# Neighbourhood-attention and Fourier encoder layer: first token tiles gated from Y in place, prompt weight remainders on VectorE, three small reorderings

## The chip, the core and the metric

The kernel runs on one core of one Trainium2 chip. The time is device microseconds for one execution. Before the change the median of 3 runs is 946.03 us (943.36 to 946.63).

The core's engines work side by side, each on its own queue of instructions in order: TensorE (in the profile PE for the matmuls, PEld for the loading of weights), VectorE (DVE), ScalarE (ACT), GpSimd (POOL), and SyncE (SP), which here does nothing but issue DMAs.

## The reference

One encoder layer is applied to a prompt of 256 tokens and a sample of 2048 tokens, each of width 1024, with the same weights. All arrays are float32.

```python
def rms_norm(x, g):
    inv = lax.rsqrt(jnp.mean(x * x, axis=-1, keepdims=True) + RMS_EPS)
    return x * inv * g

def fourier_mix(u, w_f, b_f):
    ug = u.reshape(b, s, F_GROUPS, F_GROUP_DIM)            # 8 groups of 64
    spec = jnp.fft.fft2(ug, axes=(1, 3), norm='ortho')
    return spec.real.reshape(b, s, F_WIDTH) @ w_f + b_f    # width 512

def encoder_layer(x, w_in, rpb, w_fourier, b_fourier, g_pre, g_na, g_f, w_out, g_post):
    h = rms_norm(x, g_pre)
    q, k, v, z_a, u_f, z_f = split(h @ w_in)               # six parts of width 512
    y_a = neighbourhood_attention(q, k, v, rpb)            # 8 heads of 64, windows of 8 x 16 on a grid 64 wide
    y_f = fourier_mix(u_f, w_fourier, b_fourier)
    mixed = jnp.concatenate([rms_norm(y_a, g_na) * jax.nn.silu(z_a),
                             rms_norm(y_f, g_f) * jax.nn.silu(z_f)], axis=-1)
    return x + rms_norm(mixed @ w_out, g_post)
```

## The kernel before

**Products.** Every operand of a large product is kept as a high part (a copy in the type fp32r, mostly made by ScalarE) and a remainder (operand minus high part, mostly made by VectorE). A product is then three matmuls: high by high, high by remainder, remainder by high (`mm3`, L171 to L174). Results come into one of eight PSUM banks, which are dealt out by tag: three banks "a", two "b", one "c", two "t".

**Stages.** Prompt and sample are one row of 2304 tokens (`T`), the prompt first (`TP` = 256).

1. *Prompt stage, to about 125 us.* The projections v and u of the prompt and of two blocks of the sample are made by steps `c` (loop at L706). `x_split(c)` splits a token tile; `diag` and `diag_group` write the tokens' norm factors on diagonals (ScalarE, L327), which PE transposes into rows (`spread`, L321) for the scaling of later tiles. `r_sum` (L467) makes sums of weights on VectorE. Then 16 steps `b` make the other projections of the prompt, one weight block of 128 x 1024 each. `b_raw` (L575) splits the block two steps ahead: copy on ScalarE (L578), remainder (L579) on VectorE or, for the four steps of `WP`, on GpSimd. Beside that VectorE scales token tiles (`n_scale`, L417), adds them (`n_sum`, L440) and splits them (`n_first`, L446), and at the end splits the first weights of the next stage (`op_split`, L495).
2. *Sample projections, to about 555 us.* Seven products of half blocks stand for eight, for each of 16 weight pairs.
3. *Fourier mix, to about 610 us.* After the transform along tokens, `y_mm(e, ti)` (L1248) makes one of four channel blocks `e` and one of three column blocks `ti`, taken in the order 2, 0, 1, in two banks. `y_out` (L1262) copies the first bank with the bias by ScalarE (L1264), and VectorE puts sums and differences with the second bank in place in Y (L1272), a tile of 128 channels x 2304 tokens. The prompt's 256 tokens come out of `ti` = 2 (L1296 and L1297). Y goes to DRAM (`yD`), its squares are added up for the norm (ScalarE and GpSimd, L1332 to L1340). In the last block, `e` = 3, the scores of the first two attention groups, `G[0]` and `G[1]`, lie between the products.
4. *Attention and the Fourier half of the output, to about 847 us.* 36 groups (4 head pairs x 9) run in a pipeline of steps `k`: `transp` (L1479) transposes a group's weights by PE into the banks `ptb` and copies them to SBUF, `scores` (L1162) makes the next group's logits, `bias_max` and `exps` the softmax, `pv` the product with v, `run_squares` the squares for the norm. In every second step `f_mm` (L1442) multiplies a tile of 128 tokens of gated Y by the lower half of `w_out`, in two halves of 512 columns (12 matmuls each), and `f_evac` (L1453) scales them by the norm's factor, which `f_norm` (L1465) has summed by PE.
5. *Attention half and residual, to the end.* 18 tiles: `a_mm`, `evac` (L1678), the last norm and `residual` (L1707); the last tile is written out in `last_tile` (L1719).

**The first token tiles.** Tile 0 (tokens 0 to 127) is not loaded like the others. The prompt part of each Y goes to `yD` (L1298). In block `e` = 2 the first three blocks of tile 0 are loaded back into `y0` (L1317) with the gate Z (L1318), and GpSimd multiplies them (L1320); the fourth block is multiplied by VectorE straight from Y (L1349). ScalarE copies the high part (L1351), VectorE makes the remainder (L1353), together `y0h`. Then `y0` is loaded again for tile 1 (L1357 and L1358), which GpSimd gates later (L1409). `f_mm` of tile 0 uses `ptb[0]` for its first half and the bank "c" for its second.

**What sets the order.** PE's order is that of the program text everywhere. On ScalarE, VectorE, GpSimd and SyncE it is that of the text in the stages 1 and 2 (L602 to L961) and from the last Y block on (L1342); in between a planner orders them by its own costs and priorities. A tile of a pool waits for a free slot: Y has three slots, the squares of L1339 two.

## Time and profile before

| | |
|---|---|
| median of 3 runs | 946.03 us (943.36 to 946.63) |
| the profiled execution | 947.1 us, of which its span from first to last instruction is 945.3 us |
| mean granted TensorE clock | 0.995 of full speed |
| VectorE, ScalarE, GpSimd busy | 670.4, 470.3, 343.7 us |
| DMA | 265.02 MB, mean 280 GB/s |

A row of a timeline holds: start in us, length in us, engine, line of the program, operation, the tile written <- the tiles read (buffer numbers left out), partitions x elements and type, the count if rows are merged, and in brackets the engine's idle time just before, with what ended it. A length is that of one instruction from its start to its end; the next of the same engine often starts a little earlier, since instructions overlap by about 0.1 us. For merged rows the length runs over all of them. Matmuls overlap more: 128x512 ones start about 0.23 us apart and are 0.39 us long at full clock. "issue" is a wait for nothing that the profile shows. The chain of waits is followed back from the last instruction, at each step to what released it.

### The profile page before, as it was taken

How to read it: one execution, taken by the hardware profiler on the slowest of the kernel's cores; microseconds unless marked ns; L12 is line 12 of the kernel's file. 1: busy time of each engine (PE TensorE's matmuls, PEld its weight loads, DVE VectorE, ACT ScalarE, POOL GpSimd, SP SyncE). 2: the span in 40 equal slices, each digit the busy share in tenths (PEclk: the TensorE clock that was granted, in tenths of full speed). 3: DMA queues.
4: the chain of work that ended last, by engine and by line, in shares of the span. 5: the costliest groups of instructions: out<-in, count | busy, mean ns of one | idle time of the engine just before them, and what ended most of it. 6: DMA issues, size and time to landing. Idle time of an engine off the chain costs nothing.

```text
span 945.3 us, 18908 instructions
## 1 busy us (share of the span) xinstructions
PE 929.2 (98%) x6790; PEld 777.4 (82%) x6790; DVE 670.4 (71%) x1304; ACT 470.3 (50%) x1038; POOL 343.7 (36%) x340
## 2 busy tenths in 40 slices
PE   9999999999999999999999999899999999999996
PEld 7879988888888888888888898778787887888885
DVE  5468998687864977597666545568666665659997
ACT  5747577633232643233344326457556666654443
POOL 2201302436650300363343100445456565424444
PEclk9999999999999999999999999999999999999999
DMA  8899767468573999759979788779788899869993
GB/s 307 324 354 386 242 230 299 154 247 312 205 288 151 357 396 354 275 188 324 326 275 312 256 312 280 284 232 274 243 243 271 267 288 284 268 228 373 339 344 125
DMA packets 146861, 265.02 MB, mean 280 GB/s; under 512 B 21896, under 2 KB 86664, under 8 KB 144016
## 3 DMA queue, kind: packets, MB, share of 16 engines
q1 hardware_dynamic: 146608, 263.79, 80.5%
q8 instruction: 54, 0.88, 0.4%
q14 instruction: 39, 0.32, 0.1%
q10 hardware_dynamic: 160, 0.02, 0.0%
HBM read 175.21 MB, written 95.88 MB: 287 GB/s over the span
## 4 chain that ended last, share of the span: by engine, by line
PE 83%; DMA 3%; DVE 1%; issue 1%; ACT 0%; POOL 0%; DVEq 0%; SPq 0%; ACTq 0%
PE mm L173 15%; PE mm L174 15%; PE mm L172 15%; PE ptb L1432 11%; PE po L1432 10%; PE pv L1511 5%; PE ptb L1489 3%; PE s L1181 2%; PE pab L1007 2%; PE ptb L1181 2%; DMA yD<-Y 1%; DMA wo<-woD 1%; DMA vr<-wv 0%; DMA y<-yD 0%; PE pz L174 0%
## 5 line engine op out<-in xcount | busy, mean ns | idle before, releaser
L172 PE MATMUL mm<-xh,wa 128*128 128x512 f32 x448 | 174.4, 389 | 0.0
L174 PE MATMUL mm<-xh,wa 128*128 128x512 f32 x448 | 174.3, 389 | 0.0
L173 PE MATMUL mm<-xl,wa 128*128 128x512 f32 x448 | 174.3, 389 | 0.0
L172 PEld LDWEIGHTS mm<-xh,wa 128*128 128x128 f32 x448 | 84.1, 188 | 17.5
L174 PEld LDWEIGHTS mm<-xh,wa 128*128 128x128 f32 x448 | 84.1, 188 | 17.4
L173 PEld LDWEIGHTS mm<-xl,wa 128*128 128x128 f32 x448 | 84.1, 188 | 17.4
L1432 PE MATMUL ptb<-wo,yh 128*128 128x512 f32 x272 | 86.8, 400 | 0.0
L1432 PE MATMUL po<-w,yh 128*128 128x512 f32 x280 | 86.8, 391 | 0.0
L1215 POOL TENSOR_SCALAR w<-w,m 128x352 f32<-128x352 f32 (+4 forms) x136 | 75.3, 573 | 30.7 <-PE s L1181 14.2
L549 POOL TENSOR_TENSOR ws<-wr 128x512 f32<-128x512 f32 x16 | 21.4, 1338 | 176.8 <-DMA wr<-wz 160.1
L564 DVE TENSOR_TENSOR wa<-wr,wa 128x512 fp32r<-128x512 f32 x60 | 59.9, 1005 | 31.2 <-ACT wa L563 31.2
L1208 ACT ACTIVATE w<-w,m 128x352 f32<-128x352 f32 (+4 forms) x136 | 69.9, 521 | 13.2 <-DVE m L1203 12.9
L863 DVE TENSOR_TENSOR f<-u,mm 128x512 f32<-128x512 f32 x64 | 43.6, 681 | 35.1 <-PE mm L174 30.4
L173 PE MATMUL mm<-vl,xh 128*128 128x512 f32 x168 | 65.6, 390 | 0.2 <-DVE vl L495 0.2
L174 PE MATMUL mm<-vh,xl 128*128 128x512 f32 x168 | 65.4, 389 | 0.0
L172 PE MATMUL mm<-vh,xh 128*128 128x512 f32 x168 | 65.4, 389 | 0.0
L1432 PEld LDWEIGHTS ptb<-wo,yh 128*128 128x128 f32 x272 | 49.3, 188 | 14.8 <-ACT sqa L1539 3.1
L1432 PEld LDWEIGHTS po<-w,yh 128*128 128x128 f32 x280 | 52.3, 188 | 11.0
L563 ACT CAST wa<-wr 128x512 fp32r<-128x512 f32 x60 | 36.6, 617 | 45.5 <-PE mm L174 22.1
L1511 PEld LDWEIGHTS pv<-pt,v 96*64 96x64 f32 (+2 forms) x1280 | 45.2, 137 | 11.6 <-issue 6.6
L1432 PE MATMUL po<-w,yl 128*128 128x512 f32 x140 | 54.5, 389 | 0.0
L1432 PE MATMUL ptb<-wo,yl 128*128 128x512 f32 x136 | 53.1, 390 | 0.0
(252 smaller groups left out, 2208.1 us busy)
## 6 DMA issues: line engine op xcount, KB each, us to landing
wr<-wz SPq DMA_DIRECT2D x48, 512.0 KB
vl<-sD SPq DMA_DIRECT2D x20, 512.0 KB
xm<-xm SPq DMA_DIRECT2D x9, 1024.0 KB
oD<-ofs SPq DMA_DIRECT2D x18, 512.0 KB
of<-oD SPq DMA_DIRECT2D x18, 512.0 KB
yr<-yD SPq DMA_DIRECT2D x34, 256.0 KB
zD<-f SPq DMA_DIRECT2D x16, 512.0 KB
woD<-wo SPq DMA_DIRECT2D x16, 512.0 KB
```

What stands on the lines that cost most here:

```text
L172: nc.tensor.matmul(out, lh, rh, start=first, stop=False)
L173: nc.tensor.matmul(out, lh, rl, start=False, stop=False)
L174: nc.tensor.matmul(out, ll, rh, start=False, stop=last)
L563: nc.scalar.copy(o[:, 0], src)
L564: nc.vector.tensor_tensor(out=o[:, 1], in0=src, in1=o[:, 0].bitcast(F32), op=ALU.subtract)
L863: nc.vector.tensor_tensor(out=dst(f, b), in0=src(uu[u]), in1=src(p), op=op)
L1181: nc.tensor.matmul(sp[2 * b + h][64 * y:64 * y + 64, j * w:(j + n) * w], g["q"][hs, 128 * b + 64 * y:128 * b + 64 * y + 64], kk[hs, k:k + ...
L1208: nc.scalar.activation(w, w, AF.Exp, bias=m[:, h:h + 1], scale=-1.0, accum_out=m[:, 2 + h:3 + h])
L1215: nc.gpsimd.tensor_scalar(w, w, m[:, 4 + h:5 + h], 1.0, ALU.mult, ALU.mult)
L1432: nc.tensor.matmul(p, (d["l"] if x == 2 else d["h"])[:, c], w(n, int(x == 1), c), start=j == 0, stop=j == 11)
L1489: nc.tensor.transpose(ptb[2 * b + y][:nk, x:x + 64], g["w"][b][ys, h, c0:c0 + nk], ident[ys, ys])
L1511: nc.tensor.matmul(p[hs, b, o], v[:nk, b, x, hs], g["pt"][b][:nk, h, j * 128 + o.start:j * 128 + o.stop], start=first, stop=last)
```

## The change

The change has five parts.

- The tile `y0` holds both prompt tiles (256 tokens) and stays in SBUF. Z for both is loaded once, before the first Y block; GpSimd multiplies each of the blocks 0 to 2 from Y as soon as the block's `ti` = 2 is out, VectorE the fourth. The stores of Y's prompt part, the loads of it, and the second load of Z are gone; tile 1 is gated with tile 0.
- `WP` is gone: the remainders of the steps 7, 9, 11 and 13 of the prompt are made on VectorE.
- In step `c` = 3 `x_split` of the next tile stands ahead of the diagonals.
- The first half of tile 0 in `f_mm` uses a bank "a", from which scores take theirs, in place of `ptb[0]`. In three steps of the pipeline (`k` = 9, 19, 27), where `run_squares` stands ahead of `transp`, the two copies of `transp` change engines.
- In `last_tile` the second residual of the tile before stands between the two last evacuations, and not behind both.

```diff
--- before.py
+++ after.py
@@ -26,7 +26,6 @@
 NG = 13
 NK = 16
 BP = (3, 5)
-WP = (7, 9, 11, 13)
 
 HALF = ((0, 28), (4, 8), (12, 16), (20, 24))
 KW = (24, 32, 32, 24)
@@ -576,7 +575,7 @@
         wh, wl = [gt(BS, F32R, "w" + x) for x in "hl"]
         src = wp_[b]
         nc.scalar.copy(wh, src)
-        (nc.gpsimd if b in WP else nc.vector).tensor_tensor(out=wl, in0=src, in1=wh.bitcast(F32), op=ALU.subtract)
+        nc.vector.tensor_tensor(out=wl, in0=src, in1=wh.bitcast(F32), op=ALU.subtract)
         wb[b] = wh, wl
 
 
@@ -707,12 +706,11 @@
     for c in range(3, 6):
         if c < 5:
             wz_load(3)
+        if c < 5:
+            x_split(c + 1)
         if c == 3:
             diag(0, 2)
             diag_group(0)
-        if c < 5:
-            x_split(c + 1)
-        if c == 3:
             for q in range(8):
                 r_sum(q)
         if c == 4:
@@ -1236,7 +1234,8 @@
     pg = ExitStack()
     sm = pg.enter_context(tc.tile_pool(name="smY", bufs=2))
     sqy = pq_.enter_context(tc.tile_pool(name="sqy", bufs=1, side="right"))
-    y0 = sqy.tile([128, 2, 4, 128], F32, name="y0")
+    y0 = sqy.tile([128, 2, 4, TP], F32, name="y0")
+    nc.sync.dma_start(y0[:, 1], zD[0, :, :TP].rearrange("(c p) t -> p c t", p=128))
     for t, (g, x) in enumerate(zip(G, (0, 512))):
         g["w"] = []
         for w in g["kw"]:
@@ -1295,7 +1294,6 @@
             comb(Y[:, TP + 1024:TP + 1025], slice(256, 257), ALU.subtract)
             comb(Y[:, 0:129], slice(257, 386), ALU.subtract)
             comb(Y[:, 255:128:-1], slice(258, 385), ALU.add)
-            nc.sync.dma_start(yD[1, e, :, :TP], Y[:, :TP])
 
     def first_soft(g, f=None):
         if f:
@@ -1313,11 +1311,8 @@
         if e < 3:
             for ti in (2, 0, 1):
                 y_out(e, ti, *y_mm(e, ti))
-                if e == 2 and ti == 2:
-                    nc.sync.dma_start(y0[:, 0, :3], yD[1, :3, :, :128].rearrange("c p t -> p c t"))
-                    nc.sync.dma_start(y0[:, 1], zD[0, :, :128].rearrange("(c p) t -> p c t", p=128))
-                if e == 2 and ti == 0:
-                    nc.gpsimd.tensor_tensor(out=y0[:, 0, :3], in0=y0[:, 0, :3], in1=y0[:, 1, :3], op=ALU.mult)
+                if ti == 2:
+                    nc.gpsimd.tensor_tensor(out=y0[:, 0, e], in0=Y[:, :TP], in1=y0[:, 1, e], op=ALU.mult)
             nc.sync.dma_start(yD[1, e, :, TP:], Y[:, TP:])
             if e == 0:
                 load_wo1(1)
@@ -1346,16 +1341,14 @@
         py = y_mm(e, 0)
         y0h = gt([128, 2, 4, 128], F32R, "y0h")
         y0h = [y0h[:, 0], y0h[:, 1]]
-        nc.vector.tensor_tensor(out=y0[:, 0, 3], in0=Y[:, :128], in1=y0[:, 1, 3], op=ALU.mult)
+        nc.vector.tensor_tensor(out=y0[:, 0, 3], in0=Y[:, :TP], in1=y0[:, 1, 3], op=ALU.mult)
         sq = sm.tile([128, SQ], F32, tag="sqf", name="sqf", bufs=2)
-        y_out(e, 0, *py, lambda: (nc.scalar.copy(y0h[0], y0[:, 0]),
+        y_out(e, 0, *py, lambda: (nc.scalar.copy(y0h[0], y0[:, 0, :, :128]),
                                   nc.scalar.activation(sq[:, :TP], Y[:, :TP], AF.Square)))
-        nc.vector.tensor_tensor(out=y0h[1], in0=y0[:, 0], in1=y0h[0].bitcast(F32), op=ALU.subtract)
+        nc.vector.tensor_tensor(out=y0h[1], in0=y0[:, 0, :, :128], in1=y0h[0].bitcast(F32), op=ALU.subtract)
         soft(G[0], 0)
         soft(G[0], 1)
 
-        nc.sync.dma_start(y0[:, 0], yD[1, :, :, 128:256].rearrange("c p t -> p c t"))
-        nc.sync.dma_start(y0[:, 1], zD[0, :, 128:256].rearrange("(c p) t -> p c t", p=128))
         scores(G[1])
         py = y_mm(e, 1)
         first_soft(G[1])
@@ -1440,8 +1433,11 @@
         nc.sync.dma_start(d["xt"], A["xn"][d["t"] * 128:d["t"] * 128 + 128, :])
 
     def f_mm(d, n):
-        p = d["p", n] = ptb[n if d is ftiles[0] else 2 + n] if n == 0 or d is not ftiles[0] else \
-            ps.tile([128, 512], F32, tag="c", name="pf", bufs=1)
+        if d is ftiles[0]:
+            p = ps.tile([128, 512], F32, tag="ac"[n], name="pf", bufs=3 - 2 * n)
+        else:
+            p = ptb[2 + n]
+        d["p", n] = p
         out_mm(d, n, range(12), p, lambda n, x, c: wo1[n][c][:, x])
 
     def a_mm(d, n):
@@ -1476,7 +1472,7 @@
         n = len(ds)
         rsq_ops(inva[:, ds[0]["i"]:ds[0]["i"] + n], p[:, :n], n, 1.0 / 512)
 
-    def transp(g):
+    def transp(g, swap=False):
         g["pt"] = []
         for b, ch in enumerate(g["ch"]):
             m = len(ch)
@@ -1488,7 +1484,8 @@
                         ys, x = slice(64 * y, 64 * y + 64), 64 * (h * m + j)
                         nc.tensor.transpose(ptb[2 * b + y][:nk, x:x + 64], g["w"][b][ys, h, c0:c0 + nk], ident[ys, ys])
             ov = o.rearrange("p h (j y x) -> p y h j x", y=2, x=64)
-            for y, copy in ((0, nc.scalar.copy), (1, V.tensor_copy)):
+            for y in range(2):
+                copy = V.tensor_copy if swap != (y > 0) else nc.scalar.copy
                 copy(ov[:z, y, :, :m], ptb[2 * b + y][:z, :128 * m].rearrange("p (h j x) -> p h j x", h=2, x=64))
             g["pt"].append(o)
 
@@ -1556,12 +1553,11 @@
            6: [(Y2, 1664, 2304), (Y, 1110, 1708)], 8: [(Y, 1708, 2304)]}
     ftiles[0]["h"], ftiles[0]["l"] = y0h
     y_parts(ftiles[1])
-    ftiles[1]["raw"], ftiles[1]["z"] = y0[:, 0], y0[:, 1]
+    ftiles[1]["raw"] = y0[:, 0, :, 128:]
     for x in (slice(TP, TP + 512), slice(TP + 512, T)):
         nc.sync.dma_start(yD[1, 3, :, x], Y[:, x])
     f_mm(ftiles[0], 0)
     f_norm(range(2))
-    ys_mul(ftiles[1])
     ptb += [ps.tile([128, 512], F32, tag="b", name="ptb", bufs=2) for x in range(2)]
     for x in range(2, 4):
         V.memset(ptb[x], 0.0)
@@ -1593,9 +1589,10 @@
             y = k - 24
             nc.sync.dma_start(WO[y % 2][:, y // 2].bitcast(F32), woD[0, y % 2, y // 2])
         x = k // 2
-        if k % 2 and g and i < 2:
+        first = bool(k % 2 and g and i < 2)
+        if first:
             run_squares()
-        transp(f)
+        transp(f, first)
         run_squares()
         if k % 2:
             if g:
@@ -1729,7 +1726,8 @@
                 factor(b)
                 residual(b, 0)
             evac(d, p, ns, 1 + 2 * q)
-        residual(b, 1)
+            if q == 0:
+                residual(b, 1)
         sa = d["sa"]
         V.tensor_scalar(sa[:, 0:1], sa[:, 0:1], sa[:, 1:2], None, ALU.add)
         part_sum(sa)
```

## The prediction

> **What bounds the kernel now.** I read the page's first part, then the windows, the chain of waits, and the timelines of single engines where the chain leaves TensorE (PE). The page says that PE is the bound: 16.1 of 945.3 us are without a matmul, so a change can win only in those pauses, or where PE runs slower than it could.
>
> ```profile
> PE 929.2 (98%) x6790; PEld 777.4 (82%) x6790; DVE 670.4 (71%) x1304; ACT 470.3 (50%) x1038; POOL 343.7 (36%) x340
> ```
>
> The windows show where the largest pause is (columns: stretch, its length, then busy time and count of PE, PEld, DVE, ACT, POOL, then the granted clock, DMA share, GB/s):
>
> ```profile
> 608.00:610.00 2.00, 0.39 (x3) 0.06 (x1) 0.00 (x0) 0.00 (x0) 0.61 (x1) 1.00 0.24 77
> 610.00:612.00 2.00, 0.00 (x0) 0.00 (x0) 0.94 (x4) 0.94 (x2) 0.38 (x1) 0.72 0.00 0
> 614.00:616.00 2.00, 2.00 (x6) 1.60 (x5) 1.28 (x6) 0.62 (x3) 0.83 (x3) 0.50 0.47 137
> 616.00:618.00 2.00, 2.00 (x8) 1.55 (x7) 0.00 (x0) 0.00 (x0) 0.94 (x1) 0.57 0.70 272
> ```
>
> PE stands still, the clock falls to 0.50, and work that comes afterwards runs at half rate. PE's own timeline says what that work is:
>
> ```profile
> 608.05 0.34 PE L174 MATMUL py<-abh,pql 128*128 128x384 f32 x1
> 612.53 5.40 PE L1432 MATMUL ptb<-wo,y0h 128*128 128x512 f32 x12 [4.14 <-issue]
> 617.77 0.50 PE L1468 MATMUL pfn<-ones,sqs 128*128 128x1 f32 x4
> 618.13 3.01 PE L1432 MATMUL pf<-wo,y0h 128*128 128x512 f32 x12
> 621.32 0.47 PE L1489 MATMUL ptb<-ident,sc 64*128 64x64 f32 x8 [0.18 <-DVE ofs L1463]
> ```
>
> The first token tile's first twelve matmuls start 4.14 us after the last y matmul and take 5.40 us; the same twelve for the other half, at full clock, take 3.01. The chain of waits (start, us, what) names the cause, a round trip of Y through DRAM:
>
> ```profile
> 596.65 8.90 DMA yD<-Y
> 605.63 3.69 DMA y<-yD
> ```
>
> **The changes, part by part.** *The first tile from Y.* Removed: four stores of Y's prompt part, its two loads, the gating at L1320 and L1409. Added: GpSimd gates each of the first three Y tiles where it stands (L1336's 128x256 operation, 0.73 us, is the same shape), and one load of both prompt tiles of Z ahead of them. When are the split halves of tile 0 (y0h) ready then? These rows hold the chain:
>
> ```profile
> 603.28 1.33 DVE L1272 TENSOR_TENSOR Y<-t,py 128x252 f32<-128x252 f32 x7
> 606.60 1.08 DVE L1272 TENSOR_TENSOR Y<-t,py 128x384 f32<-128x384 f32 x3
> 604.33 0.56 ACT L1264 ACTIVATE t<-py,bfs 128x384 f32<-128x384 f32 x1
> 606.38 0.29 DVE L1349 TENSOR_TENSOR y<-Y,y 128x128 f32<-128x128 f32 x1 [1.77 <-DMA y<-zD]
> 610.41 0.62 ACT L1351 CAST y0h<-y 128x512 fp32r<-128x512 f32 x1 [5.52 <-POOL y L1320]
> 611.06 0.69 DVE L1353 TENSOR_TENSOR y0h<-y,y0h 128x512 fp32r<-128x512 f32 x1 [3.39 <-ACT y0h L1351]
> 600.42 0.73 POOL L1336 TENSOR_TENSOR sqs<-sqs,sqf 128x256 f32<-128x256 f32 x1
> ```
>
> GpSimd's last operation ends at 601.15 and would end 0.73 later, 601.9, with the third gate behind it. The fourth gate, on VectorE, starts when the Y sums end (604.6), not at 606.38, since Z is there long before. It is twice as wide: at most twice 0.29, so done by 605.2. The copy on ScalarE takes 0.62 (605.8); beside it VectorE makes the next block's Y sums, 1.08 (606.3), and then the remainder, 0.69: y0h is complete at about 607.0. PE needs it at 608.05 plus 0.2, the spacing of these matmuls, so 608.25. The wait is gone with 1.2 us to spare. The bank must be free too: the change gives the first half a bank of the score pool, whose last user is evacuated by ScalarE (L1264) by 604.9.
>
> Without a pause there is no fall of the clock, so the first twelve take what the second twelve do. From start to start: idle 612.53 - 608.25 = 4.28; first half 617.77 - 612.53 = 5.24 against about 2.75 (3.01 less the tail of the last matmul), 2.49; and the transposes, which waited at 621.32 for the evacuation of a bank that they share no more, come about 0.3 earlier, at 614.2. Together **7.1 us**. What is late next is that same evacuation:
>
> ```profile
> 620.42 0.76 DVE ofs L1463
> ```
>
> It started 2.65 after the norm matmuls of 617.77. These move to 611.0, so it ends near 614.4. The scores behind the transposes take three banks of the pool in which it now lies, and start at about 614.65: 0.2 us to spare, hidden but barely; if it slips by x, I lose x - 0.2. I take the full 7.1; the ends are 5 (a 2 us wait left) and 7.4.
>
> *How the clock is counted.* In the windows the half rate lasts to about 617.6, 5 us after the matmuls resume. [...]
>
> *The prompt remainders.* Four splits of a 128x1024 weight go from GpSimd to VectorE, which in this stage has hardly a gap:
>
> ```profile
> 103.23 3.27 POOL L579 TENSOR_TENSOR wl<-wr,wh 128x1024 fp32r<-128x1024 f32 x1 [2.71 <-ACT wh L578]
> 108.99 3.07 POOL L579 TENSOR_TENSOR wl<-wr,wh 128x1024 fp32r<-128x1024 f32 x1 [2.49 <-ACT wh L578]
> 104.27 4.38 DVE L440 TENSOR_TENSOR nx<-nx 128x2048 f32<-128x2048 f32 x1
> 109.71 4.50 DVE L440 TENSOR_TENSOR nx<-nt,nx 128x2048 f32<-128x2048 f32 x1
> 114.25 2.29 DVE L440 TENSOR_TENSOR nx<-nx 128x2048 f32<-128x2048 f32 x1
> 116.45 1.22 DVE L579 TENSOR_TENSOR wl<-wr,wh 128x1024 fp32r<-128x1024 f32 x1
> 117.73 0.39 PE L174 MATMUL mm<-ph,wl 128*128 128x256 f32 x1 [1.34 <-DVE wl L579]
> 124.40 0.50 PE L173 MATMUL mm<-vl,xh 128*128 128x512 f32 x1 [0.22 <-DVE vl L495]
> ```
>
> Added: four times 1.14 (1.22 less the overlap with the next), 4.56 us on VectorE, with PE waiting behind it twice. Given back: the two sums of 4.38 and 4.50 are the same shape as the one of 2.29, and each ends just 2.15 after a GpSimd split ends (103.23 + 3.27 = 106.50, and 108.65; 108.99 + 3.07 = 112.06, and 114.21). I read this as VectorE standing still while GpSimd works. Without these splits both return to 2.29: 4.30 us. Net, VectorE is 0.26 later.
>
> [...]
>
> *x_split ahead of the diagonals.* Here PE waits for a remainder that is queued behind ten diagonals on ScalarE:
>
> ```profile
> 48.95 3.02 ACT L327 ACTIVATE dg<-onesq,invt 128x128 f32<-128x128 f32 x10
> 52.95 1.23 DVE L296 TENSOR_TENSOR xl<-xr,xh 128x1024 fp32r<-128x1024 f32 x1 [10.36 <-ACT xh L293]
> 54.23 0.50 PE L174 MATMUL mm<-wc,xl 128*128 128x512 f32 x1 [0.53 <-DVE xl L296]
> ```
>
> The remainder comes some 3 us earlier, the diagonals 1 us later, near 53.0. PE transposes them ahead of the product that waited, so it waits for the last of them instead: of 0.7 us lost I count 0.2 won. VectorE's eight sums start 3 us earlier too, but the remainder at 78.9 waits for ScalarE and a store, so between 0 and 1.1 us of that lead lives. Both parts together, PE at 124.4: from 0.5 late (the 0.26, and short waits at single weights) to 0.9 early; I take **0.1 won**.
>
> *Copies exchanged.* In three steps ScalarE squares the previous group before it copies the bank that the next scores need; one of them:
>
> ```profile
> 730.63 1.02 DVE L1492 COPY pt<-ptb 128x384 f32<-128x384 f32 x2
> 730.90 0.84 ACT L1492 COPY pt<-ptb 128x384 f32<-128x384 f32 x2
> 731.43 0.43 PE L1181 MATMUL ptb<-kk,q 64*64 64x256 f32 x1
> ```
>
> ScalarE's first copy ends at 731.32. VectorE's would end at 731.14: 0.2 earlier, and both engines are still done before the products that read all four copies. Three steps, **0.6 us**, ends 0 and 0.7.
>
> *Last residuals.* The earlier tile's second half moves ahead of the last small evacuation. VectorE's row at the end (the 128-wide evacuation is the one before):
>
> ```profile
> 938.32 0.74 DVE L1714 SCALAR_TENSOR_TENSOR of<-ptb,sr,of 128x512 f32<-128x512 f32 x1
> 938.71 0.19 ACT L1683 ACTIVATION_READ_ACCUMULATOR jk<-of 128x1 f32 x1
> 938.98 0.20 DVE L1734 TENSOR_SCALAR sa<-sa 128x1 f32<-128x1 f32 x1
> ```
>
> The final sum at 938.98 waited for ScalarE (938.90) as much as for the residual. The moved residual fits into the half microsecond that VectorE waited for PE and pushes the evacuation back by less than 0.1. I take 0, ends 0.1 lost and 0.2 won.
>
> **Sum.** 7.1 + 0.1 + 0.6 + 0 = 7.8 us. The profiled execution took 947.1 (span 945.3 and 1.8 around it), so 939.3; the median of the three runs, 946.03, lies 1.07 below it. On that median: 946.03 - 7.8 = **938.2 us**.
>
> **Rivals.** *VectorE becomes the bound of the prompt stage.* If the two long sums have another cause than GpSimd, nothing returns, and the 4.56 stand in a chain that ends at PE's wait of 124.40. For it: VectorE has no gap there. Against it: the two ends at the same distance. Time: 938.2 + 4.5 = 942.7.
>
> *A shorter wait takes the old one's place.* The third gate is behind GpSimd's adds, the copies are behind ScalarE's squares, and the evacuation has only 0.2 us. Say 2 us of waiting in all: 940.2. The clock would not fall, since here it fell only about 2.5 us into the pause (0.72 on average over 610 to 612).
>
> *Slower: the first gate waits for Z.* The planner lays out GpSimd's queue here. The first gate stands ahead of the eight adds of squares, ScalarE's squares wait for these adds, and the copy that frees PE's banks is queued behind them.
>
> ```profile
> 595.06 5.39 POOL L1340 TENSOR_TENSOR sqs<-sqs,sqf 128x288 f32<-128x288 f32 x7 [2.52 <-ACT sqf L1339]
> 581.83 1.42 SPq L1159 DMA_DIRECT2D za<-zD  x2
> 597.95 0.37 SPq L1318 DMA_DIRECT2D y<-zD  x1
> ```
>
> If Z came as late as it does now (606.3, when L1349 starts), the adds would follow two gates later, at 607.8 in place of 595.06, 12.7 us late. PE has little work in hand without free banks, some 0.7 us by my estimate: 12 us idle, and 2.5 for the clock, so 938.2 + 14.5 = 952.7. It decides at about 593.6, two gates before the seven adds. Against it: in the text of this stage the load follows the za loads, which SyncE has issued by 583.3, and the 8.4 us that it takes now (597.95 to 606.3) would end at 591.7.
>
> *The change doesn't do what it says:* something else holds the first tile as long as the load did, its weights or its bank. Nothing in the trace is that late; both are there by 605.
>
> **Chances.** Forecast 0.80; VectorE bound 0.08; a shorter wait 0.08; slower 0.03; no effect 0.01. A measurement here can tell about 0.5% from no change, 4.7 us: faster is under 941.3, slower over 950.8. The forecast's own ends, (5 or 7.4) with the small terms' ends, and 1 us for the medians (the three runs span 3.3), give 936 to 941. The range reaches up to VectorE as the bound: 936.0 to 942.8. Faster: 0.80 and most of the shorter wait, 0.86; same: 0.10; slower: 0.04.
>
> **What would show it.** Right: the windows near 608 to 614 show PE full and the clock at 1.00; the first tile's first twelve take about 3 us; no load of y from yD in the chain; L440's sums all take 2.3; the scores in the three steps start about 0.2 after their predecessors' end. Wrong: a pause of PE of over 1 us after the y matmuls, sums of L440 that still take over 4, PE's wait near 117 to 124 grown by microseconds, or GpSimd's adds starting after 595.

## The result, and the profile after

The kernel after takes 939.0 us (median of 4 runs, 937.48 to 939.44) against 946.33 (943.36 to 946.97): ratio 0.9926, interval 0.9902 to 0.995. That is 7.3 us less; forecast were 7.8 and 938.2. The profiled execution of after took 937.48 us, with a span of 935.7.

The page's first part, the row that answers to the first one of before. TensorE (PE) has 10.4 us without a matmul instead of 16.1:

```profile
PE 925.3 (99%) x6790; PEld 774.5 (83%) x6790; DVE 669.9 (72%) x1308; ACT 469.8 (50%) x1038; POOL 332.0 (35%) x337
```

The windows of after where PE stood still before (columns as in the prediction: PE, PEld, DVE, ACT, POOL, clock, DMA share, GB/s):

```profile
606.00:608.00 2.00, 2.00 (x11) 1.69 (x10) 0.87 (x5) 1.63 (x7) 1.50 (x4) 1.00 0.04 8
608.00:610.00 2.00, 2.00 (x12) 1.70 (x12) 1.00 (x7) 0.32 (x2) 0.00 (x0) 1.00 0.14 53
```

PE is full and the clock stays at 1.00; DMA is at 0.04 and 0.14: little is moved. The timeline of after over that stretch:

```profile
602.73 0.43 DVE L1344 TENSOR_TENSOR y<-Y,y 128x256 f32<-128x256 f32 x1
...
603.19 0.62 ACT L1346 CAST y0h<-y 128x512 fp32r<-128x512 f32 x1 [0.23 <-DVE y L1344]
...
604.07 0.68 DVE L1348 TENSOR_TENSOR y0h<-y,y0h 128x512 fp32r<-128x512 f32 x1
...
606.21 2.92 PE L1425 MATMUL pf<-wo,y0h 128*128 128x512 f32 x12
608.97 0.50 PE L1464 MATMUL pfn<-ones,sqs 128*128 128x1 f32 x4
609.33 3.03 PE L1425 MATMUL pf<-wo,y0h 128*128 128x512 f32 x12
...
611.72 0.75 DVE L1459 TENSOR_SCALAR ofs<-pf,invf 128x512 f32<-128x512 f32 x1
612.29 0.46 PE L1485 MATMUL ptb<-ident,sc 64*128 64x64 f32 x8
```

The last gate, the copy and the remainder are done at 604.75, 1.5 us before PE comes to the tile. The first half's twelve matmuls take 2.92, the second half's 3.03: no half rate. The evacuation ends at 612.47 and the scores behind the transposes start at 612.68: 0.21 to spare, where 0.2 was forecast.

Where the time went, by the starts of the same matmuls in the two profiled executions:

| stretch (times of the kernel before) | before | after | difference |
|---|---|---|---|
| start to the first product at full clock (9.99) | 9.99 | 8.42 | -1.57 |
| from there to the product with the prompt's last late remainder, for which PE waits on VectorE (117.73) | 107.74 | 107.01 | -0.73 |
| to the last y product (608.05) | 490.32 | 490.60 | +0.28 |
| to the first matmul of the first tile (612.53) | 4.48 | 0.18 | -4.30 |
| to the norm matmuls (617.77) | 5.23 | 2.76 | -2.47 |
| to the transposes (621.32) | 3.55 | 3.32 | -0.23 |
| to 661.7 | 40.38 | 40.56 | +0.18 |
| to 874.2 (holds the three exchanged steps) | 212.47 | 212.14 | -0.33 |
| to the last matmul (937.74) | 63.57 | 63.58 | +0.01 |
| to the end of the span | 7.56 | 7.13 | -0.43 |

The first row is the same code in both. The second needs other runs to be read: the experiments below hold the same code several times.

### The profile page after: what moved, and what is told of

It reads as the page before. It is cut to its first block, busy times and chain, and to the rows that moved or that the text cites. A ratio compares the mean times of both kernels' runs of the same rounds, so it can differ in the third digit from the quotient of the medians.

```text
span 935.7 us, 18895 instructions
## 1 busy us (share of the span) xinstructions
PE 925.3 (99%) x6790; PEld 774.5 (83%) x6790; DVE 669.9 (72%) x1308; ACT 469.8 (50%) x1038; POOL 332.0 (35%) x337
## 4 chain that ended last, share of the span: by engine, by line
PE 94%; DMA 3%; DVE 2%; issue 1%; ACT 0%; DVEq 0%; SPq 0%
PE mm L172 18%; PE mm L173 18%; PE mm L171 17%; PE ptb L1425 10%; PE po L1425 10%; PE pv L1508 5%; PE ptb L1485 3%; PE s L1179 3%; PE pab L1005 2%; PE ptb L1179 2%; DMA woD<-wo 1%; PE py L171 1%; PE py L173 1%; PE py L172 1%; PE pf L1425 1%
## 5 line engine op out<-in xcount | busy, mean ns | idle before, releaser
L563 DVE TENSOR_TENSOR wa<-wr,wa 128x512 fp32r<-128x512 f32 x60 | 57.7, 969 | 30.6 <-ACT wa L562 30.3
```

The lines of the kernel that those rows point to most:

```text
L563: nc.vector.tensor_tensor(out=o[:, 1], in0=src, in1=o[:, 0].bitcast(F32), op=ALU.subtract)
```

## The experiments

My theory: all of the gain that a median shows is the first tile's, by the wait, the half clock behind it and the shared bank; of the small parts only the exchanged copies and the moved residual win anything. Rivals: the first-tile gain was made elsewhere; the prompt stage won by the change; the bank, not Y, held the tile.

**The first tile alone.** The kernel after with the other parts undone.

```diff
+WP = (7, 9, 11, 13)
...
-        nc.vector.tensor_tensor(out=wl, in0=src, in1=wh.bitcast(F32), op=ALU.subtract)
+        (nc.gpsimd if b in WP else nc.vector).tensor_tensor(out=wl, in0=src, in1=wh.bitcast(F32), op=ALU.subtract)
...
-        transp(f, first)
+        transp(f)
...
-            if q == 0:
-                residual(b, 1)
+        residual(b, 1)
```

> The kernel after the change with every part undone but the first token tiles from Y (with the new bank). My theory: the main pause of TensorE and its half clock are this part alone, so the transposes of the first group start 7.0 us earlier than in the kernel before, counted from the last y product, and the prompt stage, the steps of the exchanged copies and the tail stand as before; 7.0 us less than before in all. Rival, that part of the gain at the transposes was made elsewhere (engines that run earlier since the prompt stage): under 6.5 here.

Measured: 939.0 us (938.55 to 940.06) against 946.07, ratio 0.9933 (0.9918 to 0.9948): as much as all parts together. From the last y product to the transposes 6.26 us, to the hundredth what after takes. The forecast's main part is this part's own. The prompt stage, with the old code, also took 107.13 instead of the 107.74 of the profile of before, so most of the 0.73 in the table above is scatter between executions.

**All other parts.** The kernel before with the prompt remainders on VectorE, the split ahead of the diagonals, the exchanged copies and the moved residual.

> The kernel before with all other parts: prompt remainders on VectorE, the split ahead of the diagonals, exchanged copies, moved residual. My theory: 0.4 to 0.8 won in the prompt stage, 0.6 in the three steps, 0.5 in the tail, so 1.5 to 1.9 less than before (counted in the trace from the first full-rate matmul on), and the pause of about 4.1 us and the half clock at the first token tile stay. By my prediction's terms it would be 0.7. Rival, that the moved residual wins nothing and the tail's 0.45 is scatter between runs: the time from the last matmul's start to the end of the span stays as before.

Measured: 945.56 us (942.71 to 946.91), ratio 0.9994 (0.9983 to 1.0005): the size is inside what can be told from no change. The trace tells the parts apart. Tail: 6.97, so 0.59 less than before; the three steps' stretch: 212.03, 0.44 less. The prompt stage took 108.31, longer than with the old code: I had expected 0.4 to 0.8 won there, and that is wrong. The pause stayed, but it cost less than in the profile of before; PE's rows:

```profile
613.62 4.52 PE L1430 MATMUL ptb<-wo,y0h 128*128 128x512 f32 x12 [4.12 <-issue]
617.98 0.50 PE L1466 MATMUL pfn<-ones,sqs 128*128 128x1 f32 x4
```

The pause is as long as before (4.12 and 4.14), but the twelve matmuls take 4.52 instead of 5.40. The clock is the reason; it is taken up below.

**The bank alone.** The kernel before, with the first half in a bank of the scores.

```diff
-        p = d["p", n] = ptb[n if d is ftiles[0] else 2 + n] if n == 0 or d is not ftiles[0] else \
-            ps.tile([128, 512], F32, tag="c", name="pf", bufs=1)
+        if d is ftiles[0]:
+            p = ps.tile([128, 512], F32, tag="ac"[n], name="pf", bufs=3 - 2 * n)
+        else:
+            p = ptb[2 + n]
+        d["p", n] = p
```

> The kernel before with the new bank alone for the first half of the first token tile. In the kernel before, that half's bank is read by the softmax's maximum until 612.42, and its first matmul starts at 612.53. My theory: the operands are there at 611.75 (end of VectorE's remainder), so the first matmul starts 0.5 to 0.8 earlier, and the transposes, which shared the bank, lose their wait of 0.18: 0.5 to 1.0 won. Rival, that the first half waited for its operands alone, as I put it in the prediction: 0.2 to 0.3 won, all at the transposes.

Measured: 944.92 us (943.25 to 947.8), ratio 0.9991 (0.9978 to 1.0003). Its timeline:

```profile
608.85 0.62 ACT L1351 CAST y0h<-y 128x512 fp32r<-128x512 f32 x1 [5.47 <-POOL y L1320]
609.50 0.69 DVE L1353 TENSOR_TENSOR y0h<-y,y0h 128x512 fp32r<-128x512 f32 x1 [3.37 <-ACT y0h L1351]
...
609.52 4.57 PE L1432 MATMUL pf<-wo,y0h 128*128 128x512 f32 x12 [2.64 <-ACT y0h L1351]
```

The first half starts as soon as ScalarE's copy is done, and VectorE's remainder comes in time behind it. In the kernel before the copy was done at 611.03 and PE started at 612.53, just behind the end of this row of VectorE (612.42; in the run "The clock by itself" below the wait's own row names the maxima, `DVE m L1203`):

```profile
612.07 0.35 DVE L1203 CUSTOM_DVE_ANT_1 sc<-ptb,tb 128x192 f32<-128x192 f32 x1
```

So 1.5 us of the pause of 4.14 was the old bank, which the softmax's maxima still read, queued on VectorE behind the tile's remainder. From the last y product to the transposes it is 10.69 against 13.26: 1.50 of that is the bank, 0.83 a shorter half rate (taken up below), 0.25 the transposes' wait. I had expected 0.5 to 0.8 here; the mechanism is right and larger, and the rival, that the tile waited for its operands alone, falls. It is what my prediction had taken for granted.

**After with the old bank.**

```diff
-            p = ps.tile([128, 512], F32, tag="ac"[n], name="pf", bufs=3 - 2 * n)
+            p = ps.tile([128, 512], F32, tag="c", name="pf", bufs=1) if n else ptb[0]
```

> The kernel after with the first token tile's first half back in its old bank. In the kernel before with the new bank alone, the first half started 1.5 us earlier against its operands than with the old one, whose last reader is the softmax's maximum. My theory: with Y gated in place the operands are so early that this reader has ended (605.76 in the kernel after) before TensorE comes to the tile (606.21), so the start stays; the transposes, which share the old bank, wait for its evacuation (612.47) and start 0.2 to 0.4 later: 0.2 to 0.4 slower than after. Rival, that the bank is a part of the 7 us by itself: the first half starts over 1 us later than after.

Measured: 938.04 us (937.77 to 939.07), ratio 0.9924 (0.9907 to 0.9941). The two rows of its timeline that matter:

```profile
611.79 0.75 DVE L1459 TENSOR_SCALAR ofs<-ptb,invf 128x512 f32<-128x512 f32 x1
...
612.69 0.46 PE L1485 MATMUL ptb<-ident,sc 64*128 64x64 f32 x8 [0.26 <-DVE ofs L1459]
```

The first half starts 0.18 behind the last y product, as in after: no wait for the bank. The transposes wait 0.26 for the evacuation and come 0.32 later than in after, and 0.12 of that is made good at the next scores. A bank that was worth 1.5 us while Y came late is worth 0.2 once Y is early: the two gains overlap, and neither can be read off by undoing one part alone.

**The clock by itself.** The kernel before with matmuls in the pause whose result is not used.

```diff
+    wm = ps.tile([128, 512], F32, tag="a", name="wm", bufs=3)
+    for x in range(17):
+        nc.tensor.matmul(wm, wo1[0][0][:, 0, :128], wo1[0][1][:, 0], start=True, stop=True)
```

> The kernel before with 17 matmuls of 128x512 added between the last y product and the first token tile, whose result nobody uses (some 3.9 us at 0.23 each): TensorE is busy through the pause, but the first token tile still comes when Y comes back from DRAM. My theory: the clock stays at 1.00, the first twelve matmuls of the tile take 2.7 to 3.0 instead of 5.4, and the kernel is 2.0 to 2.5 us faster than before although it does more. Rival A, that the first twelve are slow for another cause (their operands or weights come late one by one): they still take over 5 us and the time stays as before. Rival B, that only part of the half rate is the pause's doing: 1 to 1.5.

PE's timeline in that run:

```profile
606.90 4.05 PE L1560 MATMUL wm<-wo,wo 128*128 128x512 f32 x17
611.28 2.97 PE L1432 MATMUL ptb<-wo,y0h 128*128 128x512 f32 x12 [0.32 <-DVE m L1203]
...
696.61 0.69 PE L1181 MATMUL s<-kk,q 64*64 64x256 f32 x1 [2.46 <-issue]
```

The tile comes as late as before (4.55 behind the last y product), and its first twelve matmuls take 2.97 instead of 5.40. Start to start that is 5.23 to 2.81: 2.42 won by nothing but a busy PE. Rivals A and B fall. The whole kernel did not show it: 945.38 us (943.95 to 949.46), ratio 1.0 (0.9987 to 1.0013). The last row shows where the profiled execution lost it again: 85 us later PE stands still for 2.46 us with nothing visible to wait for, and the granted clock falls again (0.50 from 696.3 to 703.2); the stretch from 661.7 to 874.2 takes 218.33 there against 212.47. That execution, with 949.46 us, is the slowest of the ten, and what the others lost is not seen. Why PE stands still is open (see the next run).

**Bank and busy pause together.** The same with the new bank and 11 such matmuls.

> The kernel before with the new bank for the first half and 11 matmuls of 128x512 (2.5 us) ahead of it whose result nobody uses. With the new bank alone TensorE still stood still for 2.64 us and the first twelve matmuls took 4.4 at half clock; with 17 such matmuls and the old bank they took 2.8. My theory: bank (1.5) and clock (1.6) add up, what stays is the wait for Y's way through DRAM alone (2.6 to 2.9), so from the last y product to the transposes 9.0 to 9.2 instead of 13.3 in the kernel before and 6.3 in the kernel after; about 3.5 to 4 faster than before. Rival, that the clock falls even in a row of such matmuls or that the bank's gain was scatter: over 10.5 to the transposes.

From the last y product to the transposes 9.53 us (expected 9.0 to 9.2; before 13.26, after 6.26), so bank and clock add up to 3.7, and 3.3 is left for Y's way through DRAM. The median is 945.02 us (942.61 to 950.33), ratio 0.9993 (0.9979 to 1.0007): again less than the trace promised. The profile shows 0.64 lost at the next scores and 1.19 near 694, at nearly the same matmul as in the run before, again under "issue". The kernels before and after show no stall there (PE busy 10.00 of 10.00 us from 690 to 700). The cause was not shown.

**Remainders on GpSimd, beside other work.** After with the steps 7 and 9 on GpSimd again.

```diff
+WP = (7, 9)
...
-        nc.vector.tensor_tensor(out=wl, in0=src, in1=wh.bitcast(F32), op=ALU.subtract)
+        (nc.gpsimd if b in WP else nc.vector).tensor_tensor(out=wl, in0=src, in1=wh.bitcast(F32), op=ALU.subtract)
```

> The kernel after with the prompt remainders of the steps 7 and 9 on GpSimd again; they run beside VectorE's scaling of token tiles and splits, the two of steps 11 and 13 beside the sums stay on VectorE. My theory, that GpSimd and VectorE block each other in operations with two operands in SBUF: all sums take 2.3; two splits of 1.14 less on VectorE, some of it given back where a split on GpSimd meets one on VectorE; TensorE's waits between 97 and 125 us, 1.0 in all, shrink to 0.3 to 0.8, and the product of v at the stage's end comes that much earlier. Rival, that any work of GpSimd there costs VectorE as much as it takes over: the stage ends as in the kernel after.

**The same with the steps 11 and 13** (`WP = (11, 13)`).

> The kernel after with the prompt remainders of the steps 11 and 13 on GpSimd again, those beside VectorE's sums. My theory: two of the sums take 4.4 and 4.5 again, VectorE has 4.3 more for the sums and 2.3 less for the splits, and the product of v at the stage's end comes up to 2 us later than in the kernel after. Rival, that the long sums have another cause: all sums 2.3 and the stage ends 0.3 to 1 earlier, like the run with steps 7 and 9.

With 7 and 9: 936.28 us (934.8 to 938.02), ratio 0.9902 (0.9883 to 0.9922). Its timeline, one of the two steps:

```profile
95.62 1.22 DVE L579 TENSOR_TENSOR wl<-wr,wh 128x1024 fp32r<-128x1024 f32 x1
96.06 3.05 POOL L579 TENSOR_TENSOR wl<-wr,wh 128x1024 fp32r<-128x1024 f32 x1 [2.90 <-ACT wh L578]
96.76 2.72 DVE L417 SCALAR_TENSOR_TENSOR nx<-nx,gpre,iv 128x512 f32<-128x512 f32 x4
```

GpSimd's split runs beside VectorE's scaling, whose second operand `iv` is in PSUM, and the four take 2.72 in all, 0.68 each, against 1.40 for two with no split beside them (86.13): VectorE is not held up. All sums take 2.3 (the view of groups: `L440` 2288, 2287 and 2285 ns), and PE has no wait between 90 and 140 us. The expectation was too small: counted from the last u product's evacuation, the product of v comes 2.27 earlier than in after (44.90 against 47.17), not 0.3 to 0.8.

With 11 and 13: 941.64 us (939.94 to 942.52), ratio 0.9956 (0.994 to 0.9973). Its timeline:

```profile
100.55 1.23 DVE L579 TENSOR_TENSOR wl<-wr,wh 128x1024 fp32r<-128x1024 f32 x1
101.31 4.92 POOL L579 TENSOR_TENSOR wl<-wr,wh 128x1024 fp32r<-128x1024 f32 x1 [73.27 <-ACT wh L578]
101.69 2.29 DVE L440 TENSOR_TENSOR nt<-nx 128x2048 f32<-128x2048 f32 x1
...
104.01 4.36 DVE L440 TENSOR_TENSOR nx<-nx 128x2048 f32<-128x2048 f32 x1
...
107.39 3.22 POOL L579 TENSOR_TENSOR wl<-wr,wh 128x1024 fp32r<-128x1024 f32 x1 [1.17 <-ACT wh L578]
108.30 3.40 DVE L579 TENSOR_TENSOR wl<-wr,wh 128x1024 fp32r<-128x1024 f32 x1
...
111.75 0.58 PE L174 MATMUL mm<-ph,wl 128*128 128x256 f32 x1 [2.33 <-DVE wl L579]
```

Read it as turns. GpSimd's split, begun at 101.31, meets VectorE's remainder, which runs until 101.78; VectorE's sum, begun at 101.69, still goes ahead of it, to 103.98, and the split ends only at 106.23. VectorE's next sum, begun at 104.01, ends 2.14 later, at 108.37. GpSimd's second split ends at 110.61, 2.24 behind that, and VectorE's remainder, 1.22 by itself, takes 3.40 and ends 1.09 behind it. PE waits 2.33 for that. In these rows one of the two stands still until the other is through, and not always the one that began second. GpSimd stands still in the other runs too: each of the twelve splits in the rows of before, of the first tile alone and of the two runs here ends 2.24 to 2.29 behind the end of a VectorE operation with both operands in SBUF (99.11 and 96.84 in the run with the steps 7 and 9). I read that as its own length, an estimate from these ends; the rest of the 2.90 to 4.92 recorded is then waiting.

The rival (long sums of another cause) falls, and my 2 us were too small: the product of v comes 2.94 later than in after (50.11 from the last u product's evacuation, against 47.17). Measured from the same evacuation to PE's last late remainder, the stage takes 44.35 against 40.48 in after and 39.02 with the steps 7 and 9. Not all of that is VectorE's: behind the pause of 2.33 PE's first matmul is recorded with 0.58, the same shape behind the pause of 1.34 in the kernel before (117.73) with 0.39. How much of the lateness is PE's was not shown.

**An earlier lead for VectorE.** After with the split of the third weight block ahead of ScalarE's evacuation of the last u product.

```diff
         p_mm("u", c, range(4))
+        if c == 5:
+            b_raw(2)
...
-        if b < 14:
+        if 0 < b < 14:
             b_raw(b + 2)
```

> The kernel after with the split of the prompt's third weight block (copy on ScalarE, remainder on VectorE) ahead of ScalarE's evacuation of the last u product, which is TensorE's to end: in the kernel after VectorE stands still for 5.85 us behind that, and the lead of the moved token split, 2 us there, is lost. My theory: VectorE's remainder starts some 5 us earlier (near 71 instead of 76.6), keeps a lead up to 110, and TensorE's four waits of 0.2 and what waits at 115 to 122 go: the product of v 0.8 to 1.1 earlier, and the kernel 0.8 to 1.1 faster than after. Rival, that loads of weights hold VectorE next: the lead is gone by 100 and the time is that of after.

First two timelines of the kernel after, VectorE and ScalarE, which show where the lead of the moved token split ends:

```profile
74.95 0.69 ACT L350 ACTIVATE uo<-mm,invt 128x512 f32<-128x512 f32 x1 [5.16 <-DMA vN<-vo]
75.53 1.04 ACT L577 CAST wh<-wr 128x1024 fp32r<-128x1024 f32 x1
...
76.60 1.23 DVE L578 TENSOR_TENSOR wl<-wr,wh 128x1024 fp32r<-128x1024 f32 x1 [5.85 <-ACT wh L577]
```

ScalarE is free for `uo` some 2 us earlier than with the old order and waits there. My expectation called that a wait for PE; the row names the store of `vo`, and the row is right: PE ended the u product at 73.7, 1.2 us earlier. `uo` goes into the slot of the `vo` one step before, whose store was issued at 66.77 and let go 8.2 us later; with the old order (the run of the first tile alone) it was issued at 68.75 and let go 6.3 us later, at 75.09. The lead is lost in a store that takes longer by as much. The DMA engines are full there in both runs (share 0.98 to 1.07 from 62 to 76 us in after, 1.00 and 0.98 from 60 to 70 and to 80 with the old order). `uo` starts 66.3 to 68.0 us after PE's first product at full clock in eight runs with the new order, 66.3 to 67.2 in five with the old one. This is also the prompt stage's scatter between executions. Now the run with the early split:

```profile
67.78 3.59 DVE L578 TENSOR_TENSOR wl<-wr,wh 128x1024 fp32r<-128x1024 f32 x3
78.98 1.23 DVE L578 TENSOR_TENSOR wl<-wr,wh 128x1024 fp32r<-128x1024 f32 x1 [6.29 <-ACT wh L577]
```

The third remainder is made at 70.1 instead of 76.6, and the fourth at 78.98 instead of 79.23: the copy of that one is queued on ScalarE behind the same `uo`, which starts at 75.41 here. Of 6.5 us of lead 0.25 lives. Counted from `uo`, PE's product with the last late remainder comes 0.7 earlier (39.77 against 40.49); the median is 937.38 us (936.57 to 937.83), ratio 0.9912 (0.9898 to 0.9927), against 938.04 for the run with the old bank in the same series. Most of the lead is lost, as the rival had it, but not to loads of weights: to the same store. A further slot for `uo` was not tried.

**The better version beside after, in one series of runs.**

> The version with the remainders of the steps 7 and 9 on GpSimd once more beside the kernel after, in the same order of runs. My theory: the stage from the last u product's evacuation to the end of the prompt is 1.5 us shorter (39.0 against 40.5), half of that or more lives to the end: 0.7 to 1.8 faster than after. Rival, that the later stages take it all back (TensorE waits for a load near 148 us): same as after within 0.5.

> The kernel after, unchanged, for a comparison with the version above in the same series: 0.7 to 1.8 slower than that by my theory, within 0.5 by the rival.

Steps 7 and 9 on GpSimd: 937.51 us (936.79 to 937.91), ratio 0.991 (0.9895 to 0.9925). After: 939.25 (937.15 to 942.27), ratio 0.9925 (0.9908 to 0.9941). The medians are 1.7 apart, as the theory had it, the stage takes 38.47 against 40.49 (39.02 in the first run), the product of v comes 2.28 earlier (44.89 against 47.17), and the intervals overlap. The stage's gain is shown; that it all reaches the end is likely and not settled.

**Z as late as before.** After with Z loaded, and the three tiles gated, in the third block of Y.

```diff
-    nc.sync.dma_start(y0[:, 1], zD[0, :, :TP].rearrange("(c p) t -> p c t", p=128))
+    Ys = []
...
-                    nc.gpsimd.tensor_tensor(out=y0[:, 0, e], in0=Y[:, :TP], in1=y0[:, 1, e], op=ALU.mult)
+                    Ys.append(Y)
+                if e == 2 and ti == 2:
+                    nc.sync.dma_start(y0[:, 1], zD[0, :, :TP].rearrange("(c p) t -> p c t", p=128))
+                if e == 2 and ti == 0:
+                    for x in range(3):
+                        nc.gpsimd.tensor_tensor(out=y0[:, 0, x], in0=Ys[x][:, :TP], in1=y0[:, 1, x], op=ALU.mult)
```

> The kernel after with Z loaded where the kernel before loaded it, in the third block of Y, and the three gates of GpSimd together behind that. This makes my slower rival's condition true: in the kernel before Z came at 606.3, and the load took 8.4 us. If its mechanism is right, GpSimd's adds of squares stand still behind the gates, ScalarE's squares behind the adds, the evacuations of TensorE's banks behind the squares (and the fourth Y tile waits for the slot of a tile that is not gated yet), and TensorE stands still for some 10 us before 610 and runs at half clock afterwards: 10 to 15 us slower than after, about 950 us. Rival, that the planner moves the gates and banks give more slack than I counted: under 4 us slower.

Measured: 941.88 us (941.32 to 943.31), ratio 0.9959 (0.9943 to 0.9975), 2.6 slower than after in the same series (939.25). Its timeline:

```profile
605.31 2.10 POOL L1320 TENSOR_TENSOR y<-Y,y 128x256 f32<-128x256 f32 x3 [5.34 <-DMA y<-zD]
606.08 1.34 DVE L1271 TENSOR_TENSOR Y<-t,py 128x252 f32<-128x252 f32 x7 [3.90 <-POOL y L1320]
...
607.48 0.44 PE L171 MATMUL py<-abh,pqh 128*128 128x384 f32 x1 [1.34 <-DVE Y L1271]
```

Z lands at 605.3, and the gates follow. The planner had put the adds of squares ahead of them, so the adds and ScalarE's squares were not held up. What waits is VectorE, for the slot of the first Y tile, which the late gates free, and behind it PE, for 1.34 us; the granted clock stays at 1.00 (606 to 612). That is not all of it: the next scores wait 0.39 for a copy of ScalarE, and at 625.05 PE waits another 0.99, by its row for ScalarE, which had waited for GpSimd, and GpSimd for the load of Z for a later tile. Late Z is slower, as the prediction's rival said, but by another way and at a fifth of its 14.5. Gates that stand ahead of the adds with Z late were not tried.

## Why the prediction was right, and where it was not

**The main part: right in size and in its terms, incomplete in its cause.** Idle 4.28 forecast and 4.30 measured, half clock 2.49 and 2.47, transposes 0.3 and 0.23. The schedule held too: operands 1.2 us ahead forecast, 1.5 found. But the step "The chain of waits names the cause, a round trip of Y through DRAM" failed in part: the chain's last piece ahead of the tile is 1.18 us of "issue", and I gave it to the load. The run with the bank alone shows 1.5 us of the pause as the bank's. The sum came out because the change removes both; that is in part luck, since the prediction had given the old bank no part of the wait. Had it kept the old bank, the sum would still have come out but for 0.2, since Y in place brings the tile behind the bank's last reader.

**The half clock.** The windows of 0.1 us show where the half rate begins and ends. In the kernel before:

```profile
610.90:611.00 0.10, 0.00 (x0) 0.00 (x0) 0.00 (x0) 0.10 (x2) 0.00 (x0) 0.50 0.00 0
...
617.70:617.80 0.10, 0.10 (x3) 0.03 (x1) 0.00 (x0) 0.00 (x0) 0.00 (x0) 0.88 1.19 492
```

and in the run of all other parts:

```profile
613.50:613.60 0.10, 0.00 (x0) 0.01 (x1) 0.10 (x3) 0.10 (x1) 0.10 (x1) 0.50 0.00 0
...
616.90:617.00 0.10, 0.10 (x2) 0.10 (x1) 0.10 (x2) 0.00 (x0) 0.00 (x0) 0.95 0.00 0
```

That is 6.8 us in one execution and 3.4 in the other, with pauses of the same length (4.14 and 4.12); the run of the bank alone, with a pause of 2.64, has 3.4 (609.43 to 612.84, worked out from windows at 0.64 and 0.80). What sets the length was not shown. The half clock costs 2.5 us in the kernel before and 1.6 in the run of all other parts; I had counted the larger for every execution. The prediction's rival of a shorter wait took the fall from one pause, some 2.5 us into it. Counted from the end of PE's last matmul the clock fell after 2.5 us in the kernel before and in the run of the bank alone, after 4.0 in that of all other parts, and after 2.2 in the stall of the first run with added matmuls; whether a pause of 2 us leaves it at 1.00 was not shown. That the larger was counted would account for a part of what the medians lack to the sum's 7.8.

**The prompt remainders: right.** VectorE was to be 0.26 later. VectorE is what PE waits for at the end of this stage in both kernels, at the same time: from the last u product's evacuation to PE's product with the last late remainder it takes 40.49 to 40.51 in five runs of the old code and 40.48 to 40.50 in five of the new. That is 0.0, and the rival in which VectorE loses 4.5 did not come. The reason held: with no split of GpSimd beside them all sums take 2.3 (2.30 and 2.31 in after), and the 4.3 that come back pay for the 4.56 that are added. The turns at 101 to 111 us above show the same standstill: a sum of 4.36 and a remainder of 3.40 beside a split, against 2.29 and 1.22. Scaling with one operand in PSUM was not held up: 2.72 for four beside a split of GpSimd, with the steps 7 and 9. So two of the four splits need not have moved at all; the trace of before shows it too (2.72 for the four at 92.21, beside the split at 91.66), and the version with the steps 7 and 9 uses it.

**The token split: the lower end of what I allowed for its lead.** I counted 0.2 won and said that between 0 and 1.1 of the lead lives. None lives: ScalarE's next copy is queued behind an evacuation that waits for a store, and the store, issued 2.0 us earlier, was let go at 74.95 against 75.09. The prediction named "ScalarE and a store" and did not ask which of the two would take the lead. The 0.2 cannot be seen either: PE's wait of 0.53 is there in two of the five runs with the old order and in none of the nine with the new, but PE comes to the end of the last u product 65.0 us after its first product at full clock on average, against 65.2, with a scatter of 1.1.

**The copies: right.** At the three steps the score that waited starts 0.19, 0.22 and 0.25 earlier, 0.66 against 0.6. One of the rows of after, where the wait for ScalarE's copy stood before:

```profile
721.93 1.02 DVE L1489 COPY pt<-ptb 128x384 f32<-128x384 f32 x2
...
722.23 0.84 ACT L1489 COPY pt<-ptb 128x384 f32<-128x384 f32 x2
...
722.54 0.43 PE L1179 MATMUL ptb<-kk,q 64*64 64x256 f32 x1
```

Over the whole stretch 0.4 is left (212.54 on average in three runs of the old copies, 212.12 in nine of the new): some runs with the new copies wait 0.2 to 0.36 at a step between, for which I have no cause.

**The last residuals: the term that was mis-sized.** It was 0; it is 0.50 (7.60 from the last matmul to the end on average in five runs with the old order, 7.10 in nine with the new one). The step that failed is "The final sum at 938.98 waited for ScalarE (938.90) as much as for the residual". In the kernel before ScalarE had read the second of the sum's two columns here:

```profile
938.05 0.19 ACT L1683 ACTIVATION_READ_ACCUMULATOR jk<-of 128x1 f32 x1
```

The tail of after:

```profile
928.28 0.74 DVE L1711 SCALAR_TENSOR_TENSOR of<-ptb,sr,of 128x512 f32<-128x512 f32 x1
...
928.89 0.19 ACT L1680 ACTIVATION_READ_ACCUMULATOR jk<-of 128x1 f32 x1
928.94 0.34 DVE L1677 SCALAR_TENSOR_TENSOR of<-pl,inva,of 128x128 f32<-128x128 f32 x1
929.20 0.20 DVE L1732 TENSOR_SCALAR sa<-sa 128x1 f32<-128x1 f32 x1
...
929.59 0.19 ACT L1680 ACTIVATION_READ_ACCUMULATOR jk<-of 128x1 f32 x1
```

The sum at 929.20 starts right behind the evacuation, while ScalarE's last accumulator is read only at 929.59. The sum adds two columns, the second of which was there at 938.24 in the kernel before, 0.74 ahead of the sum (in after at 929.08); the last column enters later, in `guess`. In the kernel before the sum had waited for the residual alone. I took two things that ended close together for two conditions, without asking which operands the instruction has.

**Sum.** By the runs: 6.1 to 7.0 for the first tile, 0 for the prompt, 0.4 and 0.5, so 7.0 to 7.9; the medians say 7.3. The small terms cannot be seen in medians: the first tile alone, without them, also measures 939.0.

## What to carry to other kernels

Before a wait is given to one cause, list everything that the waiting instruction needs, its output's bank too, and the time at which each was free: two causes that end 1.5 us apart look like one in the chain of waits, and undoing either alone misprices both. When work moves from one engine to another, ask what runs beside it at that moment and where that work has its operands; here two of four moves were right and two had no reason. And a lead on one engine is worth nothing if the next instruction in its queue, or in the queue of the engine that feeds it, waits for something that the lead does not move.

## What the runs showed of the hardware

Half clock (0.50) lasted 6.8 us in the kernel before (610.9 to 617.7) and in the first run with added matmuls (696.3 to 703.2), 3.4 us in the run of all other parts (613.5 to 616.9) and in that of the bank alone (609.4 to 612.8). Behind pauses of 4.14 and 4.12 us it cost 2.5 us in the kernel before and 1.6 in the run of all other parts. Pauses of 1.34 us (late Z, and at 117.73 in the kernel before) left the granted clock at 1.00; in pauses of 2.46 (the first run with added matmuls), 2.64 (the bank alone), 4.12 and 4.14 it fell. An instruction's length in the profile can hold waiting: VectorE's remainder of 1.22 was recorded with 3.40 beside a split, GpSimd's split, some 2.3 by my estimate from the rows' ends, with 2.90 to 4.92. Matmuls added to fill a pause were followed, 85 us later, by stalls of 2.46 and 1.03 us under "issue" in the two kernels that had them; PE has none from 690 to 700 in before and after, and the cause was not shown. A store that was issued at 66.77 instead of 68.75 was let go 8.2 us after its issue instead of 6.3 (after, and the first tile alone).
